# Score products, masks and row length in the stick-breaking attention of a hybrid decoder layer

## The chip, the cores and the metric

The kernel runs on one core of one Trainium2 chip. A core has five engines with a queue each, which run beside each other and wait for each other through semaphores: TensorE (PE in the profile; its weight loads are PEld), VectorE (DVE), ScalarE (ACT), GpSimd (POOL) and SyncE (SP), which here issues DMAs only. The metric is the device time of one execution in microseconds (us).

## The reference, cut to what matters

One layer: RMSNorm, one projection of the normed tokens, four branches, gates, an output projection, then an MLP. The change lies in branch C, stick-breaking attention (8 heads of 64 channels), and in the row length of the normed tokens:

```python
z = jnp.einsum('bqhd,bkhd->bhqk', q_blk, kh) * scale
log_keep = jnp.where(mask, jax.nn.log_sigmoid(-z), 0.0)
between = lax.cumsum(log_keep, axis=3, reverse=True) - log_keep
A = jnp.where(mask, jnp.exp(jax.nn.log_sigmoid(z) + between), 0.0)
return jnp.einsum('bhqk,bkhd->bqhd', A, vh)
```

The mask is strictly causal. 1024 tokens and 16 meta tokens make 1040 positions.

## The kernel before, in words

The tokens are stored in reversed order, so that a query block j of 128 tokens looks at the columns j x 128 to 1039, and the running product over later keys is a scan from left to right. Values that need more accuracy than one pass of fp32r gives are held as a high and a low half; a projection multiplies high by high, high by low and low by high (L99 to L101).

**The normed tokens** lie in `h_hi` and `h_lo`, eight channel tiles of 128 partitions by LP columns each, LP being 1040 rounded up to a multiple of 32, so 1056. Projections go over them in pieces of 512 columns (QCH), or of 352, 352 and 336 (KCH, CCH).

**A pair of heads** is an object of class Pair. `put_q` splits the queries into tiles `qs` of 128 partitions, high half in one head's 64 partitions and low half in the other 64. `put_k` copies the high half of the keys into both halves of a tile `kh` and the low half into the head's own 64 partitions of a tile `kl`, one tile for both heads. `put_v` writes the values to `vt`, and `values` turns them into token rows `vv` with nine 128-column transposes.

**A step** is one query block of one head, 64 in all, over n = 1040, 912, 784, 656, 528, 400, 272 or 144 columns. `scores` cuts n into pieces (3, 2, 2, 2, 2, 1, 1, 1 of them). For each piece PE computes `qs` by `kh` over 128 partitions (L296) and adds `qs` by `kl` over 64 partitions (L297); ACT writes a sigmoid of the negative score to `keep` (L299), shifted by a column, and one of the score to `sig` (L300). POOL multiplies the first 128 columns of `sig` by a triangle `maskf` (L303). DVE scans `keep` (L304): running product, then a maximum with `maski`, which is 1 on the masked part of the diagonal block, so the running product is 1 there. DVE multiplies `sig` by `keep` (L306). In the next step `turn` transposes `sig` on PE (L316), ACT copies the high half, DVE subtracts the low half (`split`, L74 and L75); after two steps `combine` multiplies with `vv` (L329).

**Order.** The loop over i takes parts of step i (scores), i-1 (turn) and i-2 (combine) in turn, and after each part `spend` lays out about 1400 columns of `fill`: the projection of the next pair, or of a convolution tile under the last pair. The framework then places each instruction in its engine's queue; each queue runs in order.

`loc` has two buffers each of the tags "a" and "b": token blocks before the attention, convolution tiles later.

Of the kernel before, what the change touches and what calls it, by code (L numbers as in the profile page):

```python
# [10 lines left out]
F32 = mybir.dt.float32  # L11
F32R = mybir.dt.float32r
# [5 lines left out]
P = 128  # L18
D = 1024
# [1 line left out]
T = 1024  # L21
NM = 16
L = T + NM
LP = -(-L // 32) * 32
NB = T // P
BW = 512
HEADS = 4
# [4 lines left out]
WINDOWS = (2, 4, 8, 16)  # L32
FILL = 1400
QCH = [(0, 512), (512, 512)]
KCH = [(0, 352), (352, 352), (704, 336)]
CCH = [(0, 352), (352, 352), (704, 322)]
FCH = [(0, 256), (256, 256), (512, 256), (768, 272)]
CT_HQ, CT_HF, CT_HI, CT_HG, CT_PV = 0, 4, 8, 12, 16
CT_SQ, CT_SK, CT_SV, CT_CH, CT_CB, CT_CC, CT_G = 20, 24, 28, 32, 36, 40, 44
# [3 lines left out]

@with_exitstack
def hybrid_trunk_kernel(ctx: ExitStack, tc: tile.TileContext, x_tok, metas, vecs, gains, w_in, w_br, w_pool,
                        w_o, w_up, w_dn, lvl_mask, sb_mask, out):
    nc = tc.nc

    def pool(name, bufs=1, side=None, stack=ctx):
# [148 lines left out]
    with ExitStack() as st:  # L198
        pl = pool("attn", 1, None, st)
        VW = (NB + 1) * P  # L200
        maskf = new(pl, [P, P], F32, "maskf")
        maski = new(pl, [P, LP], F32, "maski")
        nc.gpsimd.memset(maski[:, P:], 0.0)
        sig = [new(pl, [P, VW], F32, f"sig{i}") for i in range(2)]
        keep = [new(pl, [P, L], F32, f"keep{i}") for i in range(2)]
        for i in range(2):
            nc.gpsimd.memset(sig[i], 0.0)
            nc.gpsimd.memset(keep[i][:, 0:1], 1.0)
        vt = new(pl, [P, VW], F32, "vt")
        nc.gpsimd.memset(vt[:, L:], 0.0)  # L210
        A, B = slice(0, 64), slice(64, 128)
        sides = ((A, B), (B, A))

        def tokens_load(grp):
            tiles = []
# [23 lines left out]
        class Pair:  # L239
            def __init__(self, pr):  # L240
                self.pr = pr
                self.qs, self.kh = ([new(pl, [P, w], F32R, tag, 4) for _ in range(2)]
                                    for w, tag in ((T, "qs"), (LP, "kh")))
                self.kl = new(pl, [P, LP], F32R, "kl", 2)

            def put_q(self, c0, n, ps):
                cs = slice(c0, c0 + n)
# [3 lines left out]

            def put_k(self, c0, n, ps):
                cs = slice(c0, c0 + n)
                for kh, (own, oth) in zip(self.kh, sides):
                    nc.scalar.copy(kh[own, cs], ps[own])
                    nc.scalar.copy(kh[oth, cs], ps[own])
                    nc.vector.tensor_sub(self.kl[own, cs], ps[own], kh[own, cs].bitcast(F32))

            def put_v(self, c0, n, ps):
                nc.scalar.copy(vt[:, c0:c0 + n], ps)  # L260

            def project(self):
                yield from project_steps(CT_SQ + self.pr, QCH, self.put_q)
# [1 line left out]
                yield from project_steps(CT_SV + self.pr, KCH, self.put_v)  # L265

            def values(self):
                self.vv = [new(pl, [P, NB + 1, P], F32R, "vv", 2) for _ in range(2)]
                self.br = new(loc, [P, L], F32, "b")[:, :T]
                for b0 in range(0, NB + 1, 4):  # L270
                    nb = min(4, NB + 1 - b0)
                    ps = bank("tr").rearrange("p (b c) -> p b c", c=P)[:, :nb]
                    for b in range(nb):
                        nc.tensor.transpose(ps[:, b, :], vt[:, (b0 + b) * P:(b0 + b + 1) * P], ident)
                    for vv, (own, oth) in zip(self.vv, sides):
                        bs = slice(b0, b0 + nb)
                        nc.scalar.copy(vv[:, bs, own], ps[:, :, own])
                        nc.vector.tensor_sub(vv[:, bs, oth], ps[:, :, own], vv[:, bs, own].bitcast(F32))
                yield True

        class Step:
# [4 lines left out]

            def scores(self, i):
                n, e, j, pair = self.n, self.e, self.j, self.pair
                cw = n if n <= 512 else -(-n // (32 * -(-n // 512))) * 32
                sg, kp = self.sg, _ = sig[i % 2], keep[i % 2]  # L290
                lhs = pair.qs[e][:, j * P:(j + 1) * P]
                for c0 in range(0, n, cw):
                    w = min(cw, n - c0)
                    z = bank("z")[:, :w]
                    ks = slice(j * P + c0, j * P + c0 + w)
                    nc.tensor.matmul(z, lhs, pair.kh[e][:, ks], start=True, stop=False)  # L296
                    nc.tensor.matmul(z, lhs[sides[e][0]], pair.kl[sides[e][0], ks], start=False, stop=True)  # L297
# [38 lines left out]
                yield True  # L336

        grps = [(0, 1), (2, 3), (4, 5), (6, 7), (8,)]
        g1, junk = new(pl, [P, D], F32, "kl", 2), new(pl, [P, D], F32R, "qs", 4)
# [754 lines left out]
def _layout(i):  # L1094
    i = {k: np.asarray(v) for k, v in i.items()}

    def rows(w):
        r, c = w.shape
        return np.ascontiguousarray(w.reshape(r // P, P, c // P, P).transpose(2, 1, 0, 3))

    def cols(v):
        return v.reshape(-1, P).T

    vecs = np.concatenate([cols(i["hg_norm_g"][0]), cols(i["pool_scale"][0]),
                           i["conv_w"][0].reshape(3, 4, P).transpose(2, 1, 0).reshape(P, 12),
                           cols(i["lb_logits"][0])], axis=1)
    gains = np.stack([np.broadcast_to(g, (P, D)) for g in (i["norm1_g"][0], i["norm2_g"][0], i["final_norm_g"])])
    q = np.arange(P)
    sb_mask = np.where(q[None, :] > q[:, None], 1.0, 0.0).astype(np.float32)
    return {  # L1110
        "x_tok": i["x"][0, ::-1].reshape(NB, P, D),
        "metas": i["meta_tokens"][::-1],
        "vecs": vecs,
        "gains": gains,
        "w_in": rows(i["w_in"][0]),
        "w_br": np.stack([rows(w) for w in i["w_branch"][0]]),
        "w_pool": i["pool_w"][0].reshape(4, P, 1, P),
        "w_o": i["w_o"][0].reshape(KD // 2, 2, P, 2, 512).transpose(3, 0, 2, 1, 4),
        "w_up": rows(i["w_up"][0]),
        "w_dn": i["w_down"][0].reshape(NF, P, D),  # L1120
        "lvl_mask": _level_masks(),
        "sb_mask": sb_mask,
    }


# [19 lines left out]
```

## Time and profile before

| | before |
|---|---|
| time, median of 3 runs | 2067.47 us (2066.17 to 2067.6) |
| the profiled execution | 2063.22 us, of which the span is 2061.4 us |
| PE busy | 1987.7 us, 96% of the span |
| DVE busy | 1352.9 us, 66% |
| ACT busy | 867.7 us, 42% |
| POOL busy | 411.8 us, 20% |

Busy time of PE counts a matmul until its last result is out, so two matmuls that follow each other overlap. How fast PE goes is read from the starts. The attention lies between 62 and 381 us of the span; the norm and the first projections lie ahead of it, the recurrence, the pooling and convolution, the gates, the output projection and the MLP behind it.

### The profile page before, as it was taken

Reading aid. Unit: us, or ns where it says so; the run is one execution under the profiler, and the core shown is the slowest. Engines: PE = TensorE matmul, PEld = TensorE weight load, DVE = VectorE, ACT = ScalarE, POOL = GpSimd, SP = SyncE. Lnnn points to the kernel's source line nnn. Section 1 sums busy time; section 2 is a strip of 40 time slices with the busy share of each in tenths; the row PEclk is TensorE's granted clock in tenths of the full one; section 3 lists DMA queues with packets and bytes.
Section 4 is the critical chain, followed back from the end, with each engine's and each line's share of the span. In section 5 each row is a group of like instructions: output and inputs, shape, how many; then the busy total and the mean of one; then the engine's idle time right before and its main releaser. Section 6 shows DMA issues by size and latency. Waiting matters only on the chain. (4 is left out here: it accounts for less than half of the span.)

```text
span 2061.4 us, 25709 instructions
## 1 busy us (share of the span) xinstructions
PE 1987.7 (96%) x9972; PEld 1660.1 (81%) x9972; DVE 1352.9 (66%) x1750; ACT 867.7 (42%) x1481; POOL 411.8 (20%) x310
## 2 busy tenths in 40 slices
PE   7999999999999989999999999998999999999998
PEld 6778787888889888788887788887788888778876
DVE  6677877668777973433433567479455556988887
ACT  6566665423332332433433212154444543434445
POOL 2111111200110311432330000005323320422222
PEclk9999999999999999999999999999999999999999
DMA  3100001101101122323224655142454457343443
GB/s 136 41 31 22 31 21 32 57 31 42 52 21 42 64 75 72 123 102 123 103 102 158 246 189 174 66 140 80 118 169 143 144 172 245 133 149 132 151 141 135
DMA packets 110058, 216.81 MB, mean 105 GB/s; under 512 B 7904, under 2 KB 58720, under 8 KB 109936
## 3 DMA queue, kind: packets, MB, share of 16 engines
q1 hardware_dynamic: 55840, 171.61, 24.6%
q10 hardware_dynamic: 54096, 43.56, 6.4%
q8 instruction: 78, 1.28, 0.3%
q14 instruction: 44, 0.36, 0.1%
HBM read 153.79 MB, written 61.34 MB: 104 GB/s over the span
## 5 line engine op out<-in xcount | busy, mean ns | idle before, releaser
L99 PE MATMUL mm<-h_hi,hi 128*128 128x352 f32 (+5 forms) x1008 | 360.7, 359 | 2.5 <-ACT go L886 1.9
L101 PE MATMUL mm<-h_hi,lo 128*128 128x352 f32 (+5 forms) x1008 | 348.5, 346 | 5.3 <-DVE lo L75 5.3
L100 PE MATMUL mm<-h_lo,hi 128*128 128x352 f32 (+5 forms) x1008 | 348.8, 346 | 0.4 <-DVE h_lo L75 0.4
L99 PEld LDWEIGHTS mm<-h_hi,hi 128*128 128x128 f32 x1008 | 191.5, 190 | 29.0 <-issue 10.6
L101 PEld LDWEIGHTS mm<-h_hi,lo 128*128 128x128 f32 x1008 | 191.2, 190 | 19.4 <-DVE lo L75 6.0
L100 PEld LDWEIGHTS mm<-h_lo,hi 128*128 128x128 f32 x1008 | 191.9, 190 | 14.1 <-DVE h_lo L75 1.0
L75 DVE TENSOR_TENSOR sl<-sf,sh 128x1024 fp32r<-128x1024 f32 x60 | 74.6, 1245 | 113.3 <-ACT sh L74 113.1
L75 DVE TENSOR_TENSOR lo<-raw,hi 128x1024 fp32r<-128x1024 f32 x79 | 104.8, 1326 | 62.4 <-ACT hi L74 52.4
L74 ACT CAST hi<-raw 128x1024 fp32r<-128x1024 f32 x79 | 82.9, 1049 | 115.0 <-PE mm L100 71.7
L630 POOL TENSOR_TENSOR sf<-raw 128x512 f32<-128x512 f32 x30 | 41.4, 1381 | 322.2 <-DMA raw<-in_w_up_dram 131.4
L303 POOL TENSOR_TENSOR sig<-sig,maskf 128x128 f32<-128x128 f32 x64 | 42.5, 664 | 308.1 <-ACT sig L300 215.5
L99 PE MATMUL mm<-b_hi,eh 128*128 128x512 f32 x256 | 99.6, 390 | 1.6 <-DVE mixed L792 1.6
L100 PE MATMUL mm<-b_lo,eh 128*128 128x512 f32 x256 | 100.1, 391 | 0.1
L101 PE MATMUL mm<-b_hi,el 128*128 128x512 f32 x256 | 99.6, 390 | 0.5 <-DVE el L75 0.5
L653 PE MATMUL mm<-th,sh 128*128 128x512 f32 x240 | 94.5, 394 | 5.2 <-ACT cc L658 5.2
L599 POOL TENSOR_TENSOR eh<-h_hi,h_lo 128x512 f32<-128x512 f32 x16 | 28.1, 1757 | 339.2 <-ACT hi L74 302.9
L653 PE MATMUL mm<-th,sl 128*128 128x512 f32 x240 | 94.3, 393 | 0.0
L653 PE MATMUL mm<-tl,sh 128*128 128x512 f32 x240 | 94.2, 392 | 0.0
L304 DVE TENSOR_TENSOR_SCAN keep<-keep,maski 128x1039 f32<-128x1039 f32 (+3 forms) x64 | 88.7, 1391 | 8.2 <-ACT keep L299 7.7
L74 ACT CAST sh<-sf 128x1024 fp32r<-128x1024 f32 x60 | 62.9, 1051 | 72.7 <-PE z L653 34.7
L75 DVE TENSOR_TENSOR at_l<-tr,at_h 128x384 fp32r<-128x384 f32 (+2 forms) x112 | 62.7, 568 | 27.5 <-ACT at_h L74 26.7
L75 DVE TENSOR_TENSOR el<-raw,eh 128x512 fp32r<-128x512 f32 x30 | 32.0, 1067 | 70.7 <-ACT eh L74 61.3
(386 smaller groups left out, 5029.1 us busy)
## 6 DMA issues: line engine op xcount, KB each, us to landing
raw<-in_w_in_dram SPq DMA_DIRECT2D x76, 512.0 KB, 3.6
s_raw<-sum_dram SPq DMA_DIRECT2D x28, 896.0 KB, 4.8
gate_dram<-go ACTq DMA_DIRECT2D x32, 512.0 KB, 2.6
go<-gate_dram SPq DMA_DIRECT2D x32, 512.0 KB, 3.4
raw<-in_w_up_dram SPq DMA_DIRECT2D x32, 512.0 KB, 4.1
raw<-in_w_dn_dram SPq DMA_DIRECT2D x31, 512.0 KB, 4.9
sum_dram<-go ACTq DMA_DIRECT2D x52, 256.0 KB, 4.6
sum_dram<-sums ACTq DMA_DIRECT2D x39, 256.0 KB, 4.6
```

Source lines behind the costliest of these rows:

```text
L74: nc.scalar.copy(hi, src)
L75: (eng or nc.vector).tensor_sub(lo, src, hi.bitcast(F32))
L99: nc.tensor.matmul(ps, lh, rh, start=first, stop=False)
L100: nc.tensor.matmul(ps, lh, rl, start=False, stop=False)
L101: nc.tensor.matmul(ps, ll, rh, start=False, stop=last)
L303: nc.gpsimd.tensor_mul(sg[:, :P], sg[:, :P], maskf)
L304: nc.vector.tensor_tensor_scan(kp[:, 1:n], kp[:, 1:n], maski[:, :n - 1], 1.0, op0=ALU.mult, op1=ALU.max)
L599: nc.gpsimd.tensor_add(dst, hi[:, kk, c0:c0 + 512].bitcast(F32), lo[:, kk, c0:c0 + 512].bitcast(F32))
L630: nc.gpsimd.tensor_add(s12[:, 0], a21, a22)
L653: nc.tensor.matmul(ps, lhs[i][x][:, k, :], rhs[i][y][:, k, :], start=fresh and k == 0 and n == 0, stop=k == 3 and n == 2, skip_group_check ...
```

## The change

Five things change. The second score product runs over all 128 partitions: `kl` becomes four tiles that are allocated once, two for each of two pairs in turn, whose other 64 partitions are set to zero at the start (`clear`). The masks go: POOL writes 1.0 on the masked part of `keep` and 0.0 on that of `sig` by affine selects, and the scan takes `keep` as its second operand too with a minimum. LP becomes a multiple of 64, so 1088, and the pieces become 384, 384, 272 (projections) and multiples of 64 (scores). `vt` becomes a tile of `loc`, tag "a"; the last value block is transposed over its 16 columns only. The mask's DMA, two mask tiles and their set-up go.

```diff
-LP = -(-L // 32) * 32
+LP = -(-L // 64) * 64
-KCH = [(0, 352), (352, 352), (704, 336)]
-CCH = [(0, 352), (352, 352), (704, 322)]
+KCH = [(0, 384), (384, 384), (768, 272)]
+CCH = [(0, 384), (384, 384), (768, 258)]
...
-        maskf = new(pl, [P, P], F32, "maskf")
-        maski = new(pl, [P, LP], F32, "maski")
-        nc.gpsimd.memset(maski[:, P:], 0.0)
...
-        vt = new(pl, [P, VW], F32, "vt")
-        nc.gpsimd.memset(vt[:, L:], 0.0)
...
+        kls = [new(pl, [P, LP], F32R, f"kl{i}") for i in range(4)]
+        vvs = [new(pl, [P, NB + 1, P], F32R, f"vv{i}") for i in range(2)]
+
+        def clear():
+            for i, t in enumerate(kls):
+                nc.gpsimd.memset(t[sides[i % 2][1]].bitcast(F32), 0.0)
+            for t in vvs:
+                nc.gpsimd.memset(t[:, NB, :].bitcast(F32), 0.0)
...
-                self.kl = new(pl, [P, LP], F32R, "kl", 2)
+                self.kl = kls[pr % 2 * 2:pr % 2 * 2 + 2]
+                self.vt = new(loc, [P, L], F32, "a")
...
-                    nc.vector.tensor_sub(self.kl[own, cs], ps[own], kh[own, cs].bitcast(F32))
+                    nc.vector.tensor_sub(kl[own, cs], ps[own], kh[own, cs].bitcast(F32))
...
-                cw = n if n <= 512 else -(-n // (32 * -(-n // 512))) * 32
+                cw = n if n <= 512 else -(-n // (64 * -(-n // 512))) * 64
...
-                    nc.tensor.matmul(z, lhs[sides[e][0]], pair.kl[sides[e][0], ks], start=False, stop=True)
+                    nc.tensor.matmul(z, lhs, pair.kl[e][:, ks], start=False, stop=True)
...
-                nc.gpsimd.tensor_mul(sg[:, :P], sg[:, :P], maskf)
-                nc.vector.tensor_tensor_scan(kp[:, 1:n], kp[:, 1:n], maski[:, :n - 1], 1.0, op0=ALU.mult,
-                                             op1=ALU.max)
+                for t, fill in ((kp[:, 1:P + 1], 1.0), (sg[:, :P], 0.0)):
+                    nc.gpsimd.affine_select(out=t, in_=t, compare_op=ALU.is_gt, fill=fill, base=0,
+                                            pattern=[[1, P]], channel_multiplier=-1)
+                nc.vector.tensor_tensor_scan(kp[:, 1:n], kp[:, 1:n], kp[:, 1:n], 1.0, op0=ALU.mult, op1=ALU.min)
...
-        nc.sync.dma_start(maskf, sb_mask)
-        nc.vector.tensor_scalar(maski[:, :P], maskf, -1.0, 1.0, op0=ALU.mult, op1=ALU.add)
+        clear()
```

On PE, in the first step of the first pair's second head, before (z is the score bank, mm the next pair's projection):

```order
L316 MATMUL tr_1063<-ident_75,sig_13_106 128x128 x3
L99 MATMUL mm_1059<-h_hi_93,hi_890 128x336
L100 MATMUL mm_1059<-h_lo_94,hi_890 128x336
L101 MATMUL mm_1059<-h_hi_93,lo_891 128x336
L296 MATMUL z_1072<-kh_126,qs_124 128x352
L297 MATMUL z_1072<-kl_127,qs_124 128x352
```

and in the changed kernel, where L302 and L303 are the two score products and L323 is `turn`:

```order
L323 MATMUL tr_1086<-ident_75,sig_11_103 128x128 x3
L99 MATMUL mm_1092<-h_hi_93,hi_905 128x272
L100 MATMUL mm_1092<-h_lo_94,hi_905 128x272
L101 MATMUL mm_1092<-h_hi_93,lo_906 128x272
L302 MATMUL z_1096<-kh_127,qs_125 128x384
L303 MATMUL z_1096<-kl_16_112,qs_125 128x384
```

The products stand where they stood; the widths move, and each head has a `kl` of its own.

On DVE, at the steps with n = 272 and 144 of the second pair's first head, before (the scan is printed as SCALAR_TENSOR_TENSOR; semaphores are named by the engine that raises them):

```order
L304 SCALAR_TENSOR_TENSOR keep_15_108<-keep_15_108,maski_104 128x271 [waits Activation_49]
L306 TENSOR_TENSOR sig_13_106<-sig_13_106,keep_15_108 128x272 [waits DVE_49,Pool_49]
L257 TENSOR_TENSOR kl_1436<-mm_1734,kh_1434 64x352 [waits PE_49,Activation_49]
L75 TENSOR_TENSOR at_l_1739<-tr_1812,at_h_1738 128x4x128 [waits Activation_49]
L257 TENSOR_TENSOR kl_1436<-mm_1734,kh_1435 64x352 [waits Activation_49]
L304 SCALAR_TENSOR_TENSOR keep_16_109<-keep_16_109,maski_104 128x143 [waits Activation_49]
```

and now:

```order
L312 SCALAR_TENSOR_TENSOR keep_13_105<-keep_13_105 128x271 [waits Pool_49]
L313 TENSOR_TENSOR sig_11_103<-sig_11_103,keep_13_105 128x272 [waits DVE_49,Pool_49]
L75 TENSOR_TENSOR at_l_1799<-tr_1870,at_h_1798 128x4x128 [waits Activation_49]
L261 TENSOR_TENSOR kl_15_111<-mm_1811,kh_1485 64x384 [waits PE_49,Activation_49]
L312 SCALAR_TENSOR_TENSOR keep_14_106<-keep_14_106 128x143 [waits Pool_49]
```

The scan of a step with one piece waited for ACT and now waits for POOL.

On POOL, from the weight split ahead of the attention (lo) to its first steps, before:

```order
L75 TENSOR_TENSOR lo_137<-raw_134,hi_136 128x1024
L228 TENSOR_TENSOR at_h_198<-b_142,kl_116 128x1024
L228 TENSOR_TENSOR at_l_307<-b_196,kl_116 128x1024
L228 TENSOR_TENSOR at_h_414<-b_305,kl_116 128x1024
L303 TENSOR_TENSOR sig_13_106<-sig_13_106,maskf_103 128x128
```

and now:

```order
L75 TENSOR_TENSOR lo_138<-raw_135,hi_137 128x1024
L213 MEMSET kl_18_114 64x1088
L215 MEMSET vv_19_115 128x128
L215 MEMSET vv_20_116 128x128
L231 TENSOR_TENSOR at_h_203<-b_143,qs_117 128x1024
L231 TENSOR_TENSOR at_l_312<-b_201,qs_117 128x1024
L231 TENSOR_TENSOR at_h_419<-b_310,qs_117 128x1024
L310 AFFINE_SELECT keep_13_105<-keep_13_105 128x128
L310 AFFINE_SELECT sig_11_103<-sig_11_103 128x128
```

One memset of `kl` and two of `vv` come to stand behind the weight split (three more of `kl` ahead of it), and a step has two instructions on POOL for one.

## Rows read from the trace of the kernel before

**Rows 1.** The page: busy us, share of the span, instructions, by engine.

```profile
PE 1987.7 (96%) x9972; PEld 1660.1 (81%) x9972; DVE 1352.9 (66%) x1750; ACT 867.7 (42%) x1481; POOL 411.8 (20%) x310
```

**Rows 2.** Window of the attention: length, busy (x) of PE, PEld, DVE, ACT, POOL.

```profile
61.90:380.84 318.94, 309.46 (x1767) 248.65 (x1765) 249.15 (x343) 197.08 (x462) 42.49 (x64) 1.00 0.09 29
```

**Rows 3.** Timeline of PE around one pair of score products: start us, us, instruction.

```profile
121.02 0.32 PE L296 MATMUL z<-kh,qs 128*128 128x352 f32 x1
121.27 0.42 PE L297 MATMUL z<-kl,qs 64*128 64x352 f32 x1
121.62 0.43 PE L99 MATMUL mm<-h_hi,hi 128*128 128x352 f32 x1
121.89 0.32 PE L100 MATMUL mm<-h_lo,hi 128*128 128x352 f32 x1
122.05 0.32 PE L101 MATMUL mm<-h_hi,lo 128*128 128x352 f32 x1
```

**Rows 4.** Lines, attention: the second product; count, busy us, mean ns, idle before.

```profile
L297 PE MATMUL z<-kl,qs 64*128 64x352 f32 (+6 forms) x112 | 46.8, 417 | 0.0
```

**Rows 5.** Windows of single steps: the first and the last of 64, and one between.

```profile
61.90:67.80 5.90, 5.90 (x26) 4.01 (x25) 2.93 (x4) 5.60 (x10) 0.46 (x1) 1.00 0.33 92
108.10:116.10 8.00, 7.27 (x44) 6.01 (x44) 7.91 (x8) 6.33 (x14) 0.46 (x1) 1.00 0.12 19
375.60:380.84 5.24, 4.67 (x31) 3.87 (x29) 4.21 (x10) 2.31 (x7) 0.92 (x2) 1.00 0.00 0
```

**Rows 6.** Windows of two steps: the first and the last of 32.

```profile
61.90:72.80 10.90, 10.90 (x46) 7.23 (x45) 7.61 (x9) 9.24 (x19) 1.29 (x2) 1.00 0.18 50
372.30:380.84 8.54, 7.97 (x54) 6.84 (x52) 7.51 (x14) 3.53 (x10) 1.98 (x3) 1.00 0.27 104
```

**Rows 7.** Lines, attention: scan, product with it, mask multiply.

```profile
L304 DVE TENSOR_TENSOR_SCAN keep<-keep,maski 128x1039 f32<-128x1039 f32 (+3 forms) x64 | 88.7, 1391 | 8.2 <-ACT keep L299 7.7
L306 DVE TENSOR_TENSOR sig<-sig,keep 128x1040 f32<-128x1040 f32 (+3 forms) x64 | 49.4, 772 | 6.3 <-POOL sig L303 4.0 <-DVE keep L304 0.5
L303 POOL TENSOR_TENSOR sig<-sig,maskf 128x128 f32<-128x128 f32 x64 | 42.5, 664 | 308.1 <-ACT sig L300 215.5 <-issue 37.8 <-PE tr L316 20.1
```

**Rows 8.** Timeline of POOL ahead of the attention.

```profile
1.79 0.30 POOL masks.py:199 TENSOR_SCALAR_AFFINE_SELECT ident<-ident 128x128 f32<-128x128 f32 x1
2.02 1.06 POOL L207 MEMSET sig<- 128x1152 f32 x1
10.66 2.34 POOL L75 TENSOR_TENSOR lo<-raw,hi 128x1024 fp32r<-128x1024 f32 x1 [6.39 <-ACT hi L74]
```

**Rows 9.** Timeline of DVE and POOL around one mask multiply.

```profile
225.28 2.31 DVE L304 TENSOR_TENSOR_SCAN keep<-keep,maski 128x1039 f32<-128x1039 f32 x1
226.34 1.50 POOL L303 TENSOR_TENSOR sig<-sig,maskf 128x128 f32<-128x128 f32 x1 [4.12 <-ACT sig L300]
228.07 1.24 DVE L306 TENSOR_TENSOR sig<-sig,keep 128x1040 f32<-128x1040 f32 x1 [0.48 <-POOL sig L303]
```

**Rows 10.** Timeline of PE, 512 columns: a projection, then a branch product.

```profile
393.70 0.39 PE L101 MATMUL mm<-h_hi,lo 128*128 128x512 f32 x1
...
396.49 0.39 PE L101 MATMUL mm<-h_hi,lo 128*128 128x512 f32 x1
...
1149.71 0.39 PE L100 MATMUL mm<-b_lo,eh 128*128 128x512 f32 x1
...
1151.98 0.39 PE L101 MATMUL mm<-b_hi,el 128*128 128x512 f32 x1
```

**Rows 11.** Timeline ahead of the attention: token block 4's norm, block 6's transposes.

```profile
24.37 1.28 DVE L232 SCALAR_TENSOR_TENSOR at_l<-a,st,kl 128x1024 f32<-128x1024 f32 x1
...
34.79 0.60 PE L124 MATMUL tr<-ident,at_h 128*128 128x128 f32 x4
```

**Rows 12.** DMA issues: token loads into tag "a", KB each, median us to landing.

```profile
a<-in_x_tok_dram SPq DMA_DIRECT2D x4, 512.0 KB, 5.7
```

**Rows 13.** Lines by form, whole span: projections of 512 columns.

```profile
L99 PE MATMUL mm<-h_hi,hi 128*128 128x512 f32 x320 | 130.4, 408 | 1.9 <-ACT go L886 1.9
```

More of the change, by code (lines that the diff above doesn't have):

```diff
@@ L45, in hybrid_trunk_kernel @@
 def hybrid_trunk_kernel(ctx: ExitStack, tc: tile.TileContext, x_tok, metas, vecs, gains, w_in, w_br, w_pool,
-                        w_o, w_up, w_dn, lvl_mask, sb_mask, out):
+                        w_o, w_up, w_dn, lvl_mask, out):
     nc = tc.nc
@@ L200, in hybrid_trunk_kernel @@
         VW = (NB + 1) * P
-        maskf = new(pl, [P, P], F32, "maskf")
-        maski = new(pl, [P, LP], F32, "maski")
-        nc.gpsimd.memset(maski[:, P:], 0.0)
         sig = [new(pl, [P, VW], F32, f"sig{i}") for i in range(2)]
-        keep = [new(pl, [P, L], F32, f"keep{i}") for i in range(2)]
+        keep = [new(pl, [P, (L, LP - 16)[i]], F32, f"keep{i}") for i in range(2)]
         for i in range(2):
@@ L253, in put_k @@
                 cs = slice(c0, c0 + n)
-                for kh, (own, oth) in zip(self.kh, sides):
+                for kh, kl, (own, oth) in zip(self.kh, self.kl, sides):
                     nc.scalar.copy(kh[own, cs], ps[own])
                     nc.scalar.copy(kh[oth, cs], ps[own])
-                    nc.vector.tensor_sub(self.kl[own, cs], ps[own], kh[own, cs].bitcast(F32))
+                    nc.vector.tensor_sub(kl[own, cs], ps[own], kh[own, cs].bitcast(F32))
             def put_v(self, c0, n, ps):
-                nc.scalar.copy(vt[:, c0:c0 + n], ps)
+                nc.scalar.copy(self.vt[:, c0:c0 + n], ps)
             def project(self):
@@ L267, in values @@
             def values(self):
-                self.vv = [new(pl, [P, NB + 1, P], F32R, "vv", 2) for _ in range(2)]
+                self.vv = vvs
                 self.br = new(loc, [P, L], F32, "b")[:, :T]
@@ L271, in values @@
                     nb = min(4, NB + 1 - b0)
-                    ps = bank("tr").rearrange("p (b c) -> p b c", c=P)[:, :nb]
+                    rows = P if b0 < NB else NM
+                    ps = bank("tr").rearrange("p (b c) -> p b c", c=P)[:rows, :nb]
                     for b in range(nb):
-                        nc.tensor.transpose(ps[:, b, :], vt[:, (b0 + b) * P:(b0 + b + 1) * P], ident)
+                        c0 = (b0 + b) * P
+                        nc.tensor.transpose(ps[:, b, :], self.vt[:, c0:c0 + rows], ident)
                     for vv, (own, oth) in zip(self.vv, sides):
                         bs = slice(b0, b0 + nb)
-                        nc.scalar.copy(vv[:, bs, own], ps[:, :, own])
-                        nc.vector.tensor_sub(vv[:, bs, oth], ps[:, :, own], vv[:, bs, own].bitcast(F32))
+                        nc.scalar.copy(vv[:rows, bs, own], ps[:, :, own])
+                        nc.vector.tensor_sub(vv[:rows, bs, oth], ps[:, :, own], vv[:rows, bs, own].bitcast(F32))
                 yield True
@@ L338, in hybrid_trunk_kernel @@
         grps = [(0, 1), (2, 3), (4, 5), (6, 7), (8,)]
-        g1, junk = new(pl, [P, D], F32, "kl", 2), new(pl, [P, D], F32R, "qs", 4)
+        g1, junk = new(pl, [P, D], F32, "qs", 4), new(pl, [P, D], F32R, "qs", 4)
         loads = [tokens_load(grps[0][:1])]
@@ L1107, in _layout @@
     gains = np.stack([np.broadcast_to(g, (P, D)) for g in (i["norm1_g"][0], i["norm2_g"][0], i["final_norm_g"])])
-    q = np.arange(P)
-    sb_mask = np.where(q[None, :] > q[:, None], 1.0, 0.0).astype(np.float32)
     return {
@@ L1121, in _layout @@
         "lvl_mask": _level_masks(),
-        "sb_mask": sb_mask,
     }
```

## The prediction, written before the changed kernel was run

> **What bounds the kernel now.** I read the page's busy times first: PE is busy for 96% of the span [rows 1]. That alone says little, because overlapping matmuls count until their last result. So I went to the stretch that the change touches, the attention, as one window: 318.94 us, in which PE shows 309.46 us, DVE 249.15 us and ACT 197.08 us [rows 2]. PE leads, and DVE follows at 78%, with 70 us idle. Time that leaves PE's queue leaves the attention as long as DVE can follow. Then I read the starts on PE around one pair of score products [rows 3], since only they show its pace. In a run of products over 128 partitions a matmul of 352 columns starts 0.16 us after the last one (121.89, 122.05). Around the product over 64 partitions the pace breaks: from L296's start to L297's it is 0.25 us, from there to the next projection 0.35 us, to the one after it 0.27 us. Three matmuls take 121.89 - 121.02 = 0.87 us instead of 3 x 0.16 = 0.48 us. About 0.40 us goes with each product over 64 partitions, and there are 112 of them [rows 4].
>
> **The change part by part.** *The second product on 128 rows.* It streams the same columns, so its own time stays; if it behaves like its neighbours, 112 x 0.40 = 44.8 us go from PE's queue. What is late next is DVE. I cut the attention into its 64 steps (the first, the last and one between in [rows 5]) and let each window shrink by 0.40 us per piece, but by no more than DVE's idle time in it. The step at 108.10 has two pieces, so 0.80 us to give, and DVE is idle for 8.00 - 7.91 = 0.09 us. Such a cap binds in 27 of the 64, and 31.5 us of the 44.8 are left. With windows of two steps (the first and the last of 32 in [rows 6]), where DVE may catch up in the second what it was late in the first, 39.6 us are left; with eight steps nothing is capped. The steps are staggered by one and two, so work can slip by about one step; I take the middle of the first two, 35.5 us.
>
> *The masks.* POOL's multiply goes: 64 with a mean of 664 ns [rows 7]. Two selects a step come. The only select in the trace took 0.30 us for the same 128 x 128 in fp32 [rows 8]; the nearest instruction of the attention, the multiply, is the upper bound, 0.66 us. I take 0.30 us, the same operation and shape. POOL is busy for 42 of 319 us [rows 2], so its own time is free either way. What counts is who waits. The scan now waits for the select of `keep`. In 40 of the 64 steps the scores come in two or three pieces; the select needs the first only and is done before the last one is there, so there it costs nothing while POOL is on time. In the 24 steps with one piece it lies between ACT and the scan: 0.30 us and a handoff of 0.23 us (in rows 9 the mask multiply ends at 227.84 and DVE starts at 228.07), 0.53 us. Queued behind the scan are its product, the low halves of the transposes and the folds of `combine`, and PE waits for them in the next step. If DVE is behind anyway, nothing is lost; if all 24 show, 12.7 us. I take a quarter, 3 us.
>
> The second cost is that POOL and DVE meet. The mask multiply at 226.34 lasted 1.50 us while a scan ran, and DVE's next product started 0.48 us after the scan's end at 227.59 [rows 9]. Over the attention the product waited 4.0 us for POOL [rows 7]. With twice the POOL instructions I add another 4 us; bounds 0 (they fall into other gaps) and 128 x 0.30 = 38 us less the 4.0 paid now, so 34 us.
>
> The scan itself keeps two SBUF operands and its columns: 1391 ns on average [rows 7], no change; if a scan with the same tile twice cost or saved a tenth, it would be 9 us either way, and no row shows that.
>
> *Row length and pieces.* The columns of each projection stay the same, 1040 or 1026 in three pieces, so do the counts of copies. What could move is the pace at 512 columns. In a projection from the normed tokens thirteen starts in a row span 396.49 - 393.70 = 2.79 us, 0.2325 us a matmul; in the branch products eleven span 2.27 us, 0.227 us [rows 10]. The channel tiles of the normed tokens lie 1056 x 4 = 4224 bytes apart, which is no multiple of 256; with 1088 columns it is 4352, which is one, as for every tile that goes at 0.227. If that is the reason, 960 projections of 512 columns (320 for each of three lines [rows 13]) win 0.0055 us each, 5 us; if not, nothing. I take 3 us.
>
> *Ahead of the attention.* Three memsets of `kl` come before POOL's weight split, each at most the 1.06 us of a 1152-column one [rows 8]; the mask memset goes; POOL has 6.39 us of idle time there, which hides them. One of `kl` and two small ones stand behind the split and delay POOL's part of the norm by some 1.4 us. `vt` holds one of the two "a" buffers, so token block 6 can be loaded only when block 4's norm has ended, at 25.65 [rows 11]; 5.7 us to land [rows 12] makes 31.4, and a sum of squares and a norm (1.28 us) later its transposes are due at 34.79 [rows 11]. That is about in time. I take 1 us lost, between 0 and 3.
>
> Sum: 35.5 - 3 - 4 + 3 - 1 = 30.5 us. The profiled execution took 2063.2 us, so 2032.7 us; the median of the runs is 4.3 us above it, so I predict 2037 us.
>
> **The rivals.** *A: DVE follows altogether.* The 44.8 us come whole, and the selects hide: 44.8 + 5 - 1 = 49 us, 2018 us. For it: over eight steps DVE has room; 249 us of work against 274 us. Against: DVE runs in order and waits for ACT inside each step.
>
> *B: DVE is the bound.* The step caps hold (31.5 us), the select shows in all 24 one-piece steps (12.7 us) and the meetings with POOL cost 6 us instead of 4: with 1 us ahead, about 11 us are left, 2056 us. For it: 27 capped steps. Against: PE's queue of projections lies between the steps and lets DVE work ahead.
>
> *C: slower, through the select in DVE's path.* As the mask multiply did in rows 9, the select waits behind a scan or product that is already running, and the scan of its own step waits for it, in all 64 steps. The price is the select (0.30), the handoff (0.23) and half a scan (0.70): 1.23 us, times 64 = 79 us, against 44.8 us released: 34 us slower, 2101 us. It is slower than before from 44.8 / 64 = 0.70 us a step. For it: POOL's 1.50 us in rows 9. Against: 40 of the 64 steps give the select a whole piece of time, and a step lasts 5 us on average. The Trainium skill has this as a rule, in "SBUF — State Buffer", section "Who interferes with whom": a DVE instruction with two SBUF inputs and a GpSimd instruction that reads SBUF exclude each other, whichever came first, for its whole length. Rows 9 fit it, since the 1.50 us end just after the scan; whether a select is held in the same way no row shows.
>
> *D: the change doesn't do what it says.* The 0.40 us belongs to adding a second product onto a bank just written, not to the 64 partitions. Then it stays, and only the small terms remain: -3 - 4 + 3 - 1 = -5 us, 2072 us. Against it: the projections add 24 products onto one bank at 0.16 us [rows 3].
>
> **How the numbers follow.** Forecast 55%, with its own range of 2028 to 2046; A 18%; B 18%; C 5%; D 4%. What a measurement of this kernel can tell from no change is about 0.2%, 4 us: A, the forecast and nearly all of B are faster, 0.90; same 0.04, from the tail of B and part of D; slower 0.06. The range must take in A and most of B: 2016 to 2058 us.
>
> **What would show it.** Right: the second product at the pace of the first, with starts 0.16 to 0.18 us apart at 384 columns and no break behind it; the attention some 30 us shorter; DVE's share of it near 85 to 90%; the scan waiting for POOL in the one-piece steps for a few us in all; the later stages as long as now, but for a pace of 0.227 us at 512 columns. Wrong: a break of 0.40 us that stays (D); waits of the scan for POOL beyond 20 us (B) or 45 us (C); a select well above 0.66 us; an attention 40 us shorter (A); or an end of the first projections later than 65 us.

## The result and the profile after

| | before | after |
|---|---|---|
| time, median | 2067.53 us (2066.17 to 2069.65, 4 runs) | 2049.16 us (2045.05 to 2051.5, 4 runs) |
| the profiled execution | 2063.22 us | 2047.85 us |
| ratio of the times | | 0.9908, 95% interval 0.9889 to 0.9927 |

The changed kernel is 18.4 us faster by the medians. The forecast was 30.5 us, 2037 us. The time lies in the range of 2016 to 2058 us, and just outside the likeliest case's own range of 2028 to 2046 us.

The page's busy times of the changed kernel, which answer to [rows 1]:

```profile
PE 1948.7 (95%) x9972; PEld 1659.0 (81%) x9972; DVE 1353.6 (66%) x1749; ACT 865.4 (42%) x1481; POOL 432.5 (21%) x378
```

PE lost 39 us of busy time, DVE none. Now the timeline of PE around one pair of score products, as in [rows 3] (start us, us, instruction; L302 and L303 are the two products):

```profile
121.19 0.34 PE L101 MATMUL mm<-h_hi,lo 128*128 128x384 f32 x1
121.36 0.33 PE L302 MATMUL z<-kh,qs 128*128 128x384 f32 x1
121.53 0.33 PE L303 MATMUL z<-kl,qs 128*128 128x384 f32 x1
121.71 0.33 PE L99 MATMUL mm<-h_hi,hi 128*128 128x384 f32 x1
121.88 0.33 PE L100 MATMUL mm<-h_lo,hi 128*128 128x384 f32 x1
```

The starts are 0.17 to 0.18 us apart and the second product is a matmul like any other. The break of 0.40 us is gone. That holds beyond this one place: counted from the starts against the projections' own pace, the break is 0.40 us on average (0.38 to 0.50) in the 84 of the 112 places before where projections follow the pair directly, and 0.03 us in the 85 such places now. So the question is why 45 us of breaks gave 18 us. The attention as one window, from the first score product to the last product with the values, first of the kernel before (window, length, busy of PE, PEld, DVE, ACT, POOL; it ends later than [rows 2]) and behind it PE's waits for the product of `sig`:

```profile
61.92:384.29 322.37, 312.83 (x1789) 251.76 (x1788) 250.56 (x346) 198.30 (x465) 44.34 (x66) 1.00 0.09 29
...
PE tr L316 <- DVE sig L306: 3.4, 9, 0.7
```

and of the changed kernel, with the window of the step that answers to the second of [rows 5], and the longest waits of PE and of its weight loads (us in total, times, longest):

```profile
63.00:372.72 309.72, 278.18 (x1785) 248.21 (x1784) 250.56 (x346) 195.99 (x465) 65.23 (x131) 1.00 0.09 30
...
108.00:116.26 8.26, 6.45 (x42) 6.00 (x41) 7.75 (x8) 6.37 (x15) 1.34 (x2) 1.00 0.20 56
...
PE tr L323 <- DVE sig L313: 15.1, 14, 1.8
PE av L336 <- DVE at_l L75: 4.9, 11, 1.0
...
PEld tr L323 <- issue: 17.5, 14, 2.1
PEld av L336 <- DVE at_l L75: 10.2, 22, 1.3
```

The attention is 322.37 - 309.72 = 12.7 us shorter. PE's busy time in it fell by 34.7 us, and its idle time (length less busy) grew from 9.5 to 31.5 us: 22 us came back as waits. The largest is the one for DVE's product, from 3.4 to 15.1 us, and the weight load ahead of the same transposes stands for 17.5 us in the same places. The step at 108 lasted 8.00 us before and lasts 8.26 us now: both its breaks went, and nothing was won there. Of the remaining 10 us of the 45 I can only say that busy time counts the last matmul ahead of each stop until its result is out, so that more stops hide in it.

The lines that answer to [rows 4] and [rows 7] (busy us, mean ns, idle before, releaser):

```profile
L303 PE MATMUL z<-kl,qs 128*128 128x272 f32 (+4 forms) x112 | 36.4, 325 | 0.0
...
L312 DVE TENSOR_TENSOR_SCAN keep<-keep 128x1039 f32<-128x1039 f32 (+3 forms) x64 | 88.9, 1393 | 6.8 <-ACT keep L305 3.2 <-POOL keep L310 2.2
L313 DVE TENSOR_TENSOR sig<-sig,keep 128x1040 f32<-128x1040 f32 (+3 forms) x64 | 49.6, 776 | 3.7
...
L310 POOL TENSOR_SCALAR_AFFINE_SELECT keep<-keep 128x128 f32<-128x128 f32 x64 | 34.5, 538 | 260.2 <-ACT keep L305 225.8 <-PE tr L323 20.9 <-PE mm L101 9.2
L310 POOL TENSOR_SCALAR_AFFINE_SELECT sig<-sig 128x128 f32<-128x128 f32 x64 | 29.9, 467 | 14.6 <-ACT sig L306 12.6
```

The scan waits for POOL for 2.2 us in all, and the product's 4.0 us of waits for POOL are gone. How one wait of PE comes about, from the timeline of all engines around the second step of the second pair's second head:

```profile
187.70 2.33 DVE L312 TENSOR_TENSOR_SCAN keep<-keep 128x1039 f32<-128x1039 f32 x1 [0.35 <-ACT keep L305]
...
190.02 0.34 PE L303 MATMUL z<-kl,qs 128*128 128x400 f32 x1
190.06 0.45 DVE L261 TENSOR_TENSOR kl<-mm,kh 64x272 fp32r<-64x272 f32 x1
...
190.53 1.24 DVE L313 TENSOR_TENSOR sig<-sig,keep 128x1040 f32<-128x1040 f32 x1
191.81 0.42 DVE L340 TENSOR_TENSOR b<-av,fold 64x256 f32<-64x256 f32 x1
191.92 0.52 PE L323 MATMUL tr<-ident,sig 128*128 128x128 f32 x3 [1.55 <-DVE sig L313]
192.15 2.04 DVE L312 TENSOR_TENSOR_SCAN keep<-keep 128x911 f32<-128x911 f32 x1
```

The scan of a whole row takes 2.33 us, the product of a whole row 1.24 us, an instruction of the projections lies between, and only then can the first transposes start, though they need the row's first three blocks alone. PE had run out of other work at 190.4 and stood for 1.55 us. That can be read in two ways: DVE has too much to do, or the chain of one step (scores, scan, product, transposes, one after the other over three engines) is too long for what PE has in front of its end. The experiments below test the two.

Outside the attention: the first score product starts at 63.00 us, 1.1 us later than before; block 6's transposes start at 36.82 in place of 34.79 us. Behind it, the first product at L653 of the kernel before (L659 now) starts 13.6 us earlier than it did, the last transposes at L124 18.2 us earlier, and the span ends 15.3 us earlier.

### The profile page after: what moved, and what is told of

It is laid out like the page before. It is cut to its first block, busy times and chain, and to the rows that moved or that the text cites. A ratio compares the mean times of both kernels' runs of the same rounds, so it can differ in the third digit from the quotient of the medians.

```text
span 2046.1 us, 25941 instructions
## 1 busy us (share of the span) xinstructions
PE 1948.7 (95%) x9972; PEld 1659.0 (81%) x9972; DVE 1353.6 (66%) x1749; ACT 865.4 (42%) x1481; POOL 432.5 (21%) x378
## 5 line engine op out<-in xcount | busy, mean ns | idle before, releaser
L99 PE MATMUL mm<-h_hi,hi 128*128 128x384 f32 (+4 forms) x1008 | 352.3, 350 | 2.1 <-ACT go L892 1.9
L101 PE MATMUL mm<-h_hi,lo 128*128 128x384 f32 (+4 forms) x1008 | 347.5, 345 | 4.0 <-DVE lo L75 4.0
L100 PE MATMUL mm<-h_lo,hi 128*128 128x384 f32 (+4 forms) x1008 | 347.6, 345 | 0.7 <-DVE h_lo L75 0.7
L659 PE MATMUL mm<-th,sh 128*128 128x512 f32 x240 | 94.6, 394 | 6.6 <-ACT cc L664 6.6
L659 PE MATMUL mm<-tl,sh 128*128 128x512 f32 x240 | 94.3, 393 | 0.0
L659 PE MATMUL mm<-th,sl 128*128 128x512 f32 x240 | 94.2, 393 | 0.0
L312 DVE TENSOR_TENSOR_SCAN keep<-keep 128x1039 f32<-128x1039 f32 (+3 forms) x64 | 88.9, 1393 | 6.8 <-ACT keep L305 3.2
L310 POOL TENSOR_SCALAR_AFFINE_SELECT keep<-keep 128x128 f32<-128x128 f32 x64 | 34.5, 538 | 260.2 <-ACT keep L305 225.8
L75 DVE TENSOR_TENSOR at_l<-tr,at_h 128x384 fp32r<-128x384 f32 (+2 forms) x112 | 62.6, 567 | 22.5 <-ACT at_h L74 20.2
```

The costliest lines, as they stand in the source:

```text
L75: (eng or nc.vector).tensor_sub(lo, src, hi.bitcast(F32))
L99: nc.tensor.matmul(ps, lh, rh, start=first, stop=False)
L100: nc.tensor.matmul(ps, lh, rl, start=False, stop=False)
L101: nc.tensor.matmul(ps, ll, rh, start=False, stop=last)
L310: nc.gpsimd.affine_select(out=t, in_=t, compare_op=ALU.is_gt, fill=fill, base=0, pattern=[[1, P]], channel_multiplier=-1)
L312: nc.vector.tensor_tensor_scan(kp[:, 1:n], kp[:, 1:n], kp[:, 1:n], 1.0, op0=ALU.mult, op1=ALU.min)
```

## The experiments

The theory at the start: the second product frees PE, DVE's queue in order takes most of it back, and the selects cost little. Each time stands as a ratio to the kernel before, measured beside it on the same chip. The attention's columns are from windows like the two above, PE idle being length less PE busy.

| kernel | attention us | PE idle | DVE busy | median us | ratio, 95% |
|---|---|---|---|---|---|
| before | 322.37 | 9.5 | 250.56 | 2067.5 | 1 |
| after | 309.72 | 31.5 | 250.56 | 2049.2 | 0.9908 (0.9889 to 0.9927) |
| second product alone | 311.10 | 31.9 | 249.94 | 2060.1 | 0.9960 (0.9947 to 0.9973) |
| selects alone | 322.29 | 9.8 | 250.69 | 2069.7 | 1.0002 (0.9991 to 1.0013) |
| row length alone | 322.44 | 9.7 | 250.69 | 2066.0 | 0.9975 (0.9965 to 0.9986) |
| after, rows and pieces of before | 310.68 | 32.0 | 249.76 | 2060.5 | 0.9957 (0.9943 to 0.9970) |
| before, short scan | 307.92 | 0.7 | 197.31 | 2052.8 | 0.9924 (0.9907 to 0.9942) |
| after, short scan | 276.60 | 5.7 | 196.52 | 2017.5 | 0.9758 (0.9736 to 0.9779) |
| before, other fill | 322.10 | 8.6 | 252.81 | 2069.3 | 1.0002 (0.9992 to 1.0012) |
| after, other fill | 308.41 | 32.4 | 252.47 | 2050.6 | 0.9917 (0.9904 to 0.9930) |
| after, addition on GpSimd | 311.89 | 34.1 | 241.87 | 2051.0 | 0.9916 (0.9903 to 0.9930) |
| after, both of these | 307.76 | 31.8 | 240.49 | 2048.4 | 0.9911 (0.9895 to 0.9927) |
| after, scan by pieces | 300.64 | 23.8 | 265.33 | 2041.5 | 0.9874 (0.9854 to 0.9894) |
| the same, addition on GpSimd | 300.97 | 23.6 | 256.96 | 2041.3 | 0.9868 (0.9850 to 0.9886) |

**The second product alone.**

```diff
+        kls = [new(pl, [P, LP], F32R, f"kl{i}") for i in range(4)]
...
-                    nc.tensor.matmul(z, lhs[sides[e][0]], pair.kl[sides[e][0], ks], start=False, stop=True)
+                    nc.tensor.matmul(z, lhs, pair.kl[e][:, ks], start=False, stop=True)
...
```

> The kernel before with the second product over 128 rows alone: four key tiles padded with zeros, and, to make room for them, the values in a tile of `loc` and the last value block over its 16 columns. Masks, row length and pieces are those of before. Theory (VectorE sets the pace once TensorE is freed, the selects cost little): the attention is 10 to 16 us shorter, 1 us is lost ahead of it, so 2052 to 2059 us. Rival 1 (the selects in the scan's path took what was gained): without them the attention is 30 us shorter or more, 2037 us or less. Rival 2 (the gain in the attention came from the wider pieces of 384 columns): under 5 us of gain, 2063 us or more.

Measured: 0.9960, some 8 us (5.6 to 11); the median of 2060.1 us is just above the 2052 to 2059 expected, with 2070.0 us for the kernel before beside it. The attention alone is 11.3 us shorter, 2.2 us are lost ahead of it. That is nearly all that the whole change wins in the attention, without a select: rival 1 falls, and rival 2 too, since the pieces are those of before.

**The selects alone.**

```diff
...
-                nc.gpsimd.tensor_mul(sg[:, :P], sg[:, :P], maskf)
-                nc.vector.tensor_tensor_scan(kp[:, 1:n], kp[:, 1:n], maski[:, :n - 1], 1.0, op0=ALU.mult,
-                                             op1=ALU.max)
+                for t, fill in ((kp[:, 1:P + 1], 1.0), (sg[:, :P], 0.0)):
+                    nc.gpsimd.affine_select(out=t, in_=t, compare_op=ALU.is_gt, fill=fill, base=0,
+                                            pattern=[[1, P]], channel_multiplier=-1)
+                nc.vector.tensor_tensor_scan(kp[:, 1:n], kp[:, 1:n], kp[:, 1:n], 1.0, op0=ALU.mult, op1=ALU.min)
```

> The kernel before with the masks by affine selects alone. Theory: TensorE's queue still holds the breaks around the products over 64 partitions, so a select of 0.3 to 0.5 us in the scan's path hides: 2065 to 2071 us. Rival 1 (the selects sit in the path): slower by 5 us or more, 2073 us or above.

Measured: 1.0002 (0.9991 to 1.0013), no change beyond 2 to 3 us either way, as the theory said.

**The row length alone.**

```diff
-LP = -(-L // 32) * 32
+LP = -(-L // 64) * 64
```

> The kernel before with rows of 1088 columns alone (one number changed, all pieces as they were). Theory (channel tiles 4224 bytes apart slow the moving operand of 512 columns): the projections at 0.2325 us a matmul go to 0.227, 4 to 6 us faster, 2061.5 to 2064 us, all of it after the attention and in the fill of 512 columns. Rival (the pace has to do with the pieces or with the gates' code around it): no change, 2066 to 2069 us.

Measured: 0.9975, 5.2 us (2.9 to 7.2), the 4 to 6 us of the theory; the median of 2066.0 is above the time expected, since the kernel before itself had 2070.0 us beside it. The pace changed with this one number, as the timeline of PE shows where [rows 10] has a projection of 512 columns (thirteen starts, the first and the last):

```profile
393.74 0.39 PE L100 MATMUL mm<-h_lo,hi 128*128 128x512 f32 x1
...
396.46 0.39 PE L100 MATMUL mm<-h_lo,hi 128*128 128x512 f32 x1
```

Twelve steps in 2.72 us are 0.227 us each; before it was 0.2325. Over that stage (between the attention and L653, some 470 intervals) the median went from 0.232 to 0.227 us, and in the gates the mean went from 0.230 to 0.227.

The gates show more. There a run of products over the normed tokens goes over four channel tiles. In the kernel before, the three products over the first tile of a run start 0.227 us apart, those over the other three 0.231 on average. The first ten products right behind such a run are slow too (0.231), though they read tiles whose rows this number doesn't size, and the later ones are not (0.227). With rows of 1088 columns all go at 0.227. So the slowing begins with the second channel tile of a run, 4224 bytes after the first, and lasts beyond the run. Whether the distance between the tiles counts or the address at which the second one begins, no run separates.

**The changed kernel with rows and pieces of before.**

```diff
-LP = -(-L // 64) * 64
+LP = -(-L // 32) * 32
...
-KCH = [(0, 384), (384, 384), (768, 272)]
+KCH = [(0, 352), (352, 352), (704, 336)]
...
-                cw = n if n <= 512 else -(-n // (64 * -(-n // 512))) * 64
+                cw = n if n <= 512 else -(-n // (32 * -(-n // 512))) * 32
```

> The changed kernel with rows of 1056 columns and the old pieces (352, multiples of 32). Theory: the attention is as long as in the changed kernel within 3 us, the later stages lose 4 to 6 us, 2052 to 2057 us. Rival 2 (wider pieces made the gain in the attention): the attention is 8 us longer or more, 2060 us or above. Against the kernel with the product alone it shows the selects: theory within 3 us, rival 1 slower by 10 us or more.

Measured: 0.9957, the attention 1.0 us longer than in the changed kernel and 0.4 us shorter than with the product alone. So the selects cost nothing that shows on top of the product either. Its median of 2060.5 us is above the 2052 to 2057 expected: the distance to the changed kernel is 10 us, of which the row length explains 5.2; the profile shows 1.0 in the attention and 0.9 ahead of it. The rest is within the intervals and I leave it open.

**A short scan, in both kernels.** The edit of the changed one is shown; the running product beyond 143 columns is left out.

```diff
-                nc.vector.tensor_tensor_scan(kp[:, 1:n], kp[:, 1:n], kp[:, 1:n], 1.0, op0=ALU.mult, op1=ALU.min)
+                nc.vector.tensor_tensor_scan(kp[:, 1:144], kp[:, 1:144], kp[:, 1:144], 1.0, op0=ALU.mult, op1=ALU.min)
```

> The kernel before with the scan over 143 columns in every step instead of n - 1; the running product beyond them is left out, all else stays. That takes about 60 us of work from VectorE in the attention. Theory (TensorE's queue bound the attention before): only VectorE's few waits go, 5 to 20 us faster, 2047 to 2063 us. Rival (VectorE's queue set the pace already before): 30 us faster or more.

> The changed kernel with the same short scan; the running product beyond 143 columns is left out. Theory (TensorE was freed of some 45 us, VectorE's queue keeps most of it back): with VectorE relieved the rest comes out, so this kernel is 35 to 48 us faster than the kernel before with the short scan, 2003 to 2020 us. Rival 1 (selects and handoffs to GpSimd hold it back) or rival 3 (TensorE's own time did not shrink by 45 us): the distance between the two kernels with the short scan is that of the two kernels with the full one, 15 to 20 us.

Measured: the kernel before gains 0.76%, the changed one 2.42%. The distance between them is 35.3 us by the medians (34 ± 6 us by the ratios), not the 18 us of the two with the full scan; in the attention 31.3 us in place of 12.7 us. So PE was freed of at least that, and what held it back runs through DVE. Window and PE's longest waits of the changed kernel with the short scan:

```profile
62.40:339.00 276.60, 270.93 (x1782) 247.25 (x1780) 196.52 (x346) 197.38 (x465) 50.45 (x131) 1.00 0.10 33
...
PE tr L323 <- DVE at_l L75: 2.0, 3, 1.1
...
PE tr L323 <- DVE sig L313: 0.5, 3, 0.2
...
L312 DVE TENSOR_TENSOR_SCAN keep<-keep 128x143 f32<-128x143 f32 x64 | 29.7, 465 | 15.4 <-POOL keep L310 14.6
```

The wait for the product fell from 15.1 to 0.5 us. The short scan now waits for the select, 14.6 us in all; PE's whole idle time is 5.7 us, so most of that costs PE nothing. But a shorter scan takes away both work and length, so the two readings still stand.

**The fill laid out in another way.** If DVE has too much to do in the second step of each head and room elsewhere, PE's fill can be put where DVE is late.

```diff
-                    owed = spend(owed + FILL)
+                    owed = spend(owed + (1900 if r % NB == 1 else 1000))
```

> The kernel before with the fill laid out in another way: 1900 columns a part in the steps where VectorE's queue is fullest (the second of each head), 1000 in the others, in place of 1400 everywhere. The work is the same. Theory (TensorE's queue bound the attention before, so where its fill stands matters little): within 8 us of before, 2058 to 2074 us.

> The changed kernel with the same other layout of the fill. Theory (VectorE's queue sets the pace in the second steps of the heads, with some 14 us of waits of TensorE, and has room where the fill is thick): 8 to 20 us faster than the changed kernel, 2030 to 2042 us. Rival (VectorE is the bound throughout, the fill only covers): within 4 us of the changed kernel, 2045 to 2053 us.

Measured: 1.0002 for the kernel before, and 0.9917 for the changed one, which has 0.9908 without it. My theory expected 8 to 20 us and got 1.3 us in the attention and nothing in the time. The time is the one that the rival gave. PE's idle time is 32.4 us in place of 31.5, so this other layout, the only one tried, took none of the waits away.

**The addition of `combine` on GpSimd.**

```diff
+                dst = pair.br[own, g * 2 * P:(g + 1) * 2 * P]
                 nc.scalar.copy(fold[own], av[oth])
-                nc.vector.tensor_add(pair.br[own, g * 2 * P:(g + 1) * 2 * P], av[own], fold[own])
+                nc.scalar.copy(dst, av[own])
+                nc.gpsimd.tensor_add(dst, dst, fold[own])
```

> The changed kernel with the addition at the end of `combine` on GpSimd, 32 times, and ScalarE copying both halves. VectorE loses 13 us of work and the 15 us that it stood waiting for ScalarE's copy in front of that addition. Theory (VectorE's queue in order sets the pace): 8 to 20 us faster than the changed kernel, 2030 to 2042 us. Rival 1 (meetings with GpSimd cost VectorE as much): no gain or slower, 2047 us or more.

> The changed kernel with both, the other layout of the fill and the addition on GpSimd. Theory: the two gains overlap in part, 2018 to 2035 us. If the queue of TensorE is by then the bound, as with the short scan, not under 2012 us.

Measured: 0.9916 alone and 0.9911 with the other fill, no gain over 0.9908 in either; both theories missed, and the first run has the time of its rival. The same window, PE's wait, and DVE's low halves, and behind them two lines of the changed kernel:

```profile
63.20:375.09 311.89, 277.77 (x1785) 248.50 (x1784) 241.87 (x318) 206.38 (x496) 90.31 (x159) 1.00 0.09 30
...
PE tr L323 <- DVE sig L313: 15.7, 13, 1.8
...
L75 DVE TENSOR_TENSOR at_l<-tr,at_h 128x384 fp32r<-128x384 f32 (+2 forms) x112 | 62.9, 568 | 40.9 <-ACT at_h L74 38.4 <-PE z L303 1.6
...
L75 DVE TENSOR_TENSOR at_l<-tr,at_h 128x384 fp32r<-128x384 f32 (+2 forms) x112 | 62.6, 567 | 22.5 <-ACT at_h L74 20.2 <-PE z L303 1.6
L340 DVE TENSOR_TENSOR b<-av,fold 64x256 f32<-64x256 f32 x31 | 13.1, 422 | 15.4 <-ACT fold L339 14.8
```

The addition was 13.1 us on DVE, the scans became 3.1 us longer beside GpSimd, and in all DVE lost 8.7 us of busy time. It lost the wait ahead of its addition (15.4 us in the changed kernel) too, and the time went straight into another wait: `at_l` stands 40.9 us behind ACT's copy, which was 22.5 us in the changed kernel. ACT's copy waits for the transposes, these for the product, that for the scan. So the sum of DVE's work is not the bound. The length of the chain fits, but this run doesn't show it by itself: ACT has a second copy for each addition, 11.4 us in all, and is at it for 3.7 of the 40.9 us.

**Scan and product by pieces.** The same chain made shorter with more work on DVE: each score piece is scanned, from the last column of the piece before, and multiplied as soon as it is there. The two selects come right behind the first piece.

```diff
-                    if c0 + w < n:
-                        yield True
-                for t, fill in ((kp[:, 1:P + 1], 1.0), (sg[:, :P], 0.0)):
-                    nc.gpsimd.affine_select(out=t, in_=t, compare_op=ALU.is_gt, fill=fill, base=0,
-                                            pattern=[[1, P]], channel_multiplier=-1)
-                nc.vector.tensor_tensor_scan(kp[:, 1:n], kp[:, 1:n], kp[:, 1:n], 1.0, op0=ALU.mult, op1=ALU.min)
-                nc.vector.tensor_mul(sg[:, :n], sg[:, :n], kp[:, :n])
-                yield True
+                    if c0 == 0:
+                        for t, fill in ((kp[:, 1:P + 1], 1.0), (sg[:, :P], 0.0)):
+                            nc.gpsimd.affine_select(out=t, in_=t, compare_op=ALU.is_gt, fill=fill, base=0,
+                                                    pattern=[[1, P]], channel_multiplier=-1)
+                    kc = kp[:, c0 + 1:c0 + 1 + w1]
+                    nc.vector.tensor_tensor_scan(kc, kc, kc, kp[:, c0:c0 + 1], op0=ALU.mult, op1=ALU.min)
+                    nc.vector.tensor_mul(sg[:, c0:c0 + w], sg[:, c0:c0 + w], kp[:, c0:c0 + w])
+                    yield True
```

> The changed kernel with scan and product done piece by piece: after each score piece its columns are scanned (from the last column of the piece before) and multiplied, so VectorE starts on a step while its later pieces are still on TensorE, and the first transposes no longer wait for a whole row. VectorE gets 96 instructions more over the attention, some 5 to 10 us of extra work. Theory as it stands after the runs with less work on VectorE (what holds TensorE is the length of the chain score, scan, product, transposes, and not the sum of VectorE's work): TensorE's waits for the product, 15 us and the 17 us beside them, fall by half or more, 8 to 25 us faster than the changed kernel, 2024 to 2042 us. Rival (the sum of VectorE's work is the bound): 3 to 10 us slower, 2052 us or more.

Measured: 2041.5 us, 0.9874 against 0.9908: 7 ± 6 us faster than the changed kernel, and in the attention 9.1 us. Window, PE's longest waits, and DVE's scan and product:

```profile
62.70:363.34 300.64, 276.89 (x1786) 248.31 (x1785) 265.33 (x442) 197.02 (x465) 57.81 (x131) 1.00 0.10 31
...
PE tr L323 <- DVE at_l L75: 10.3, 11, 2.6
...
PEld tr L323 <- issue: 2.2, 6, 0.6
...
L312 DVE TENSOR_TENSOR_SCAN keep<-keep 128x271 f32<-128x271 f32 (+4 forms) x112 | 102.4, 919 | 8.9 <-POOL keep L309 7.8
L75 DVE TENSOR_TENSOR at_l<-tr,at_h 128x384 fp32r<-128x384 f32 (+2 forms) x112 | 62.4, 565 | 8.8 <-ACT at_h L74 8.1
L313 DVE TENSOR_TENSOR sig<-sig,keep 128x272 f32<-128x272 f32 (+4 forms) x112 | 56.4, 507 | 6.9 <-POOL sig L309 0.9
```

DVE works 14.8 us more and the attention is 9.1 us shorter. The wait for the product, 15.1 us, is no longer among PE's waits, and the weight loads' 17.5 us in front of the same transposes are 2.2 us. What is late next are the low halves `at_l`, for which the next transposes wait (10.3 us, before 3.1). I had expected 8 to 25 us; 7 us is at or just under the lower end. The waits for the product went, as expected, but PE's idle time fell from 31.5 to 23.8 us only, since others took their place. The rival, the sum of DVE's work, is out. One thing stays unparted: the pieces bring each product earlier, and they also hold DVE's queue for a shorter time at a stretch, so that what stands behind a scan, `at_l` too, comes sooner.

**Pieces, and the addition on GpSimd.** Now DVE is busy for 265 of 301 us, so its sum could be the bound.

> The changed kernel with scan and product piece by piece and, besides, the addition at the end of `combine` on GpSimd, which takes 13 us of work from VectorE. Without the pieces that relief was worth nothing. Theory (the pieces took the chain's length away, so that the sum of VectorE's work, 269 of 307 us, is what is left): now it is worth 4 to 12 us, 2029 to 2038 us. Rival (the bound is still a chain of waits, or meetings with GpSimd cost as much as is saved): within 3 us of the kernel with the pieces, 2039 to 2045 us.

Measured: 0.9868 against 0.9874, and 300.97 against 300.64 us in the attention: nothing again. The rival holds: 8.4 us less work on DVE are still worth nothing, and the longest wait of PE that is left is again one for DVE, for `at_l` (9.5 us). This kernel and the one with the pieces are the fastest of those that compute the whole layer, 26 to 27 us under the kernel before. A deeper stagger (turning a step's row two steps later) would lengthen what PE has in front of it; it needs a third `sig` and `keep`, for which there was no room, and wasn't tried.

## Why the prediction was right in sign and range, and where its size was off

- **The break was real.** 0.40 us with a product over 64 partitions, as predicted: the starts after show none. Rival D is out. With DVE's scan short, 31 us of the 44.8 come out in the attention, so most of that term was there; whether the rest was ever on the path is open.
- **The step that failed** is the one that says "let each window shrink by 0.40 us per piece, but by no more than DVE's idle time in it", with its middle of 35.5 us. The product alone won 11.3 us in the attention, the change 12.7. The caps took every idle microsecond of DVE as one that it could have used. Most of it was no such thing. In the kernel before these lines were there to be read: DVE's low halves of the transposes and its addition in `combine`, and ACT's copies that they wait for (ACT's two in the window of [rows 2]):

```profile
L75 DVE TENSOR_TENSOR at_l<-tr,at_h 128x384 fp32r<-128x384 f32 (+2 forms) x112 | 62.7, 568 | 27.5 <-ACT at_h L74 26.7
L333 DVE TENSOR_TENSOR b<-av,fold 64x256 f32<-64x256 f32 x31 | 13.1, 422 | 16.0 <-ACT fold L332 15.3
...
L74 ACT CAST at_h<-tr 128x384 fp32r<-128x384 f32 (+2 forms) x110 | 53.5, 498 | 35.0 <-PE tr L316 31.6 <-PE av L329 2.3
L332 ACT COPY fold<-av 64x256 f32<-64x256 f32 x30 | 11.0, 367 | 26.6 <-PE av L329 26.4
```

  That makes 43 of DVE's 72 us of idle time: DVE stood at the head of its queue for ACT, which was at its copies or stood for PE. Such idle time belongs to the chain. It did not shrink away when PE got faster: in the changed kernel the two lines have 22.5 and 15.4 us, 38 of the 43. This explains part of the miss. With the idle time of these two lines left out, the caps of the prediction give 20 us by steps and 23 us by two steps, in place of 31.5 and 39.6; the product alone won 11.3. The other 10 us stay open.
- **The range held in part by luck.** With the first term as measured, 12.7 us, and the others as predicted, the sum is 12.7 - 3 - 4 + 3 - 1 = 7.7 us, so 2060 us, outside the range of 2016 to 2058. That the time lies inside is owed to the errors in the masks and the row length, which went the other way.
- **The rivals.** Rival A is out. Rival B gave 11 us of gain with DVE as the bound, and 12.7 us in the attention are close to its number, but not by its mechanism: neither the addition moved off DVE nor the fill moved to where DVE is late changed the time, and 15 us more work in shorter pieces made it shorter. The rival that is missing is the length of the chain from score to transposes. C is out: the scans wait 2.2 us for POOL in all.
- **The masks** were priced at 3 + 4 us; the runs with them alone, and on top of the product, show nothing beyond noise. The selects took 0.54 and 0.47 us on average, within the bounds of 0.30 and 0.66. A select is held as the mask multiply was in [rows 9]. Two lines of the timeline of the changed kernel:

```profile
220.92 2.31 DVE L312 TENSOR_TENSOR_SCAN keep<-keep 128x1039 f32<-128x1039 f32 x1
221.46 1.86 POOL L310 TENSOR_SCALAR_AFFINE_SELECT keep<-keep 128x128 f32<-128x128 f32 x1 [2.46 <-ACT keep L305]
```

  The select, 0.29 us when alone, lasts until 0.09 us after the scan's end. That settles what no row showed before, and agrees with the rule that the Trainium skill gives in "SBUF — State Buffer", section "Who interferes with whom". It costs nothing in this place, because the select that is held belongs to the next step, whose scan stands behind the one that runs.
- **Row length** was priced at 3 us between 0 and 5; it is 5.2 us (2.9 to 7.2), and the run that changed this one number bears out that the rows' length is the reason; whether through the distance between the channel tiles or through where they begin, it doesn't tell. The two errors, 7 us too much for the masks and some 2 too little here, took about 9 us off the miss of 23 in the first term.
- **Ahead of the attention** 1 us was expected and 1.1 us measured, and the first projections ended before 65 us.
- **DVE's share** of the attention was to be 85 to 90%; it is 250.56 of 309.72 us, 81%: DVE's work stayed, and the attention shrank less than forecast.

## What to carry to other kernels

Before you count an engine's idle time as room, read what ended it: idle time at the head of a queue in order, waiting for an engine that waits for this one, is part of a loop, and in this kernel the loop's length counted, not the busy sum. Such a loop shows itself when work is taken off the engine and reappears at once as a wait on its next line. Then try to hand over in smaller pieces, even with more instructions: here that won 7 us, and moving work to an idle engine won nothing.

## What the runs showed of the hardware

- A product over 64 partitions in a row of products over 128 cost about 0.40 us here, spread over its own start and the two behind it; the same 112 products over 128 partitions, half of them zeros, cost none of it.
- Matmuls of 512 columns over channel tiles 4224 bytes apart went at 0.230 to 0.2325 us, over tiles 4352 bytes apart at 0.227 us, with one number of the kernel changed. The first tile of a run was not slow, and some ten matmuls over other tiles behind the run were.
- A select of 128 x 128 on GpSimd took 0.29 us alone and 1.86 us beside a scan on VectorE, until 0.09 us after the scan's end.
- Cutting 64 scans and products into 112 each added 13.5 us to the scans' times (102.4 against 88.9) and 6.8 us to the products' (56.4 against 49.6). Instructions that follow each other overlap at their ends, so DVE's busy time grew by 14.8 us, 0.15 us for each of the 96 instructions more.
